# The last third of both down projections in seven products of halves, half of its weight sums on GpSimd

## The chip, the cores and the metric

One core of a Trainium2 chip. The metric is the device time of one execution in microseconds (us); the kernel before takes 1169.24 us, the median of three runs (1168.03 to 1169.33).

## The reference

A hybrid decoder block on 528 tokens (16 learned meta tokens and 512 of input), 1024 channels, float32:

```python
h = h + 0.5 * swiglu(rmsnorm(h, ffn1_norm), w_gate1, w_up1, w_down1)
u = rmsnorm(h, mix_norm)
...
h = h + merged @ w_out
h = h + 0.5 * swiglu(rmsnorm(h, ffn2_norm), w_gate2, w_up2, w_down2)
return rmsnorm(h, final_norm)[:, 16:]

def swiglu(x, w_gate, w_up, w_down):
    return (silu(x @ w_gate) * (x @ w_up)) @ w_down
```

Between the two feed-forwards stands a token mixer (latent attention beside a gated DeltaNet), which the change leaves alone. The hidden width of a feed-forward is 2816.

## The kernel before

Activations lie transposed: channels on the 128 partitions, tokens along the free dimension (528 in the first feed-forward, 512 in the second). 1024 channels are eight such tiles, the hidden width is 22 (`FT`), numbered by `ft`. Every matrix is multiplied at higher accuracy than one pass gives: an operand x is split into hi (a cast to the matmul's format, on ScalarE) and lo = x - hi (on VectorE; `split`, L290 to L292, and L176/L177 for plain weights), and a product is three matmuls, hi hi, hi lo and lo hi (`mm3`, L204).

The function `ffn` (L303) is used for both feed-forwards. Its parts, in the order of the program:

- Plain tiles: the first `2 * nc_` hidden tiles (`NC1 = 3` pairs in the first feed-forward, `NC2 = 2` in the second) have gate and up each computed by `mm3` over eight k-tiles, 48 matmuls of 264 columns (24 of 512 in the second feed-forward). VectorE evicts them times the norm factor r (L386, L390) and multiplies gate by up (L400).
- The forms: all other gate and up tiles are made in pairs of output tiles by Strassen's scheme in Winograd's variant, a 2x2 block product in seven products instead of eight. Blocks are halves: halves of the input channels (four k-tiles each), of the tokens, and the two output tiles. For it the eight input tiles are scaled in place (L407), and for each of four pairs `k`, `k + 4` seven left-hand combinations are formed (L410 to L420): four splits and four subtractions (L413). They stay in SBUF; `xf[p][k]` is the operand of product p.
- A quad (`quad`, L442) is one pair of output tiles of gate (j = 0) or up (j = 1): it loads two raw weight tiles, forms four weight sums s1 to s4 (`side`, L427 to L429, 128x512 on VectorE), splits the seven weight operands (`form`, cast on ScalarE at L291 and difference on VectorE at L292, 128x512 each), and runs seven products of 12 matmuls (`product`, L440). Seven adds on VectorE (L433) combine them from PSUM; one product is first copied by ScalarE (L456).
- Chunks: hidden tiles are finished in three chunks, `CHUNKS1 = ((0, 8), (8, 16), (16, 22))` and `CHUNKS2 = ((0, 6), (6, 14), (14, 22))`. When a chunk is done, its activations are split (`halve`), and its share of the down projection is given out as eight down tiles (`down`, one per output tile m) between the quads of the next chunk, one after each quad; the last chunk's eight run at the end. A down tile is a plain `mm3` over the chunk's k-tiles, accumulated into the residual tile (L345).
- `finish` hands a finished output tile on: in the first feed-forward it stores it, prepares the mixer's operands and adds its square to the next norm; in the second it does the final norm. The norms' squares are added on GpSimd (L251). The last two down tiles of the second feed-forward run in token halves, so that the final norm of the first half starts early.

The program is written with the Tile framework: it allots the buffers of a tag in turn, sets the semaphores, and orders each engine's instructions by a priority that follows the order of the code. Tags that matter here: raw weights four buffers (`wraw`, `wrx`), forms eight (`whi`, `wlo`, `wex`), weight sums three (`sf`).

```python
def side(x, y, op=ALU.subtract):
    t = hid.tile([P, 4, P], F32, tag="sf", name="sf", bufs=NSF)
    nc.vector.tensor_tensor(out=t, in0=x, in1=y, op=op)
    return t
```

Of the kernel before, what the change touches and what calls it, by code (L numbers as in the profile page):

```python
# [17 lines left out]
P = 128  # L18
D = 1024
NT = 528  # L20
# [33 lines left out]
LAG = 3  # L54
NC1 = 3
NC2 = 2
CHUNKS1 = ((0, 8), (8, 16), (16, 22))
CHUNKS2 = ((0, 6), (6, 14), (14, 22))
# [3 lines left out]
NRAW = 4  # L62
NSF = 3
ORD = (2, 0, 3, 1, 4, 5, 6, 7)
ONP = (2, 3)
# [30 lines left out]
def build(tc, a, out, tap=None):  # L96
# [3 lines left out]
    with ctx:  # L100
# [24 lines left out]
        def col(name, i=0):  # L125
            return cols[:, COLS[name] + i:COLS[name] + i + 1]
# [176 lines left out]
        def ffn(wg, wd, xs, hks, wname, r, n, hid, tmp, ra, rb, hk_tile, nc_, load, finish, pre=()):  # L303
# [27 lines left out]

            two = []

            def down(c, m):
                k0, k1 = CHUNKS[c]
                k, last = k1 - k0, c == len(CHUNKS) - 1
                w, x = weights(wd[m, :, k0:k1], k), [hs[ft] for ft in range(k0, k1)]
                if c == 0:
                    hkm[m] = hk_tile(m)[:, 0:n]
                    load(m, hkm[m])  # L340
                ps = mm_tile("dn")
                hk = hkm[m]

                def acc(o, p):
                    nc.vector.scalar_tensor_tensor(out=o, in0=p, scalar=0.5, in1=o, op0=ALU.mult, op1=ALU.add)  # L345

                if last and n == SEQ and m >= KT - 2:
                    two.append((m, ps, w, hk))
                    for y in range(2 if m == KT - 1 else 0):
                        t = slice(y * h, y * h + h)  # L350
                        for m_, p_, w_, hk_ in two:
                            mm3([(p_[:, y, 0:h], y * h, y * h + h)], w_, x, True, True)
                            acc(hk_[:, t], p_[:, y, 0:h])
                            finish(m_, hk_, y)
                    return
                if n == NT:
                    mm3(outs528(ps), w, x, True, True)
                    acc(v2(hk), halves(ps))
                else:
                    mm3([(ps[:, 0, :], 0, n)], w, x, True, True)  # L360
                    acc(hk, ps[:, 0, :])
                if last:
                    finish(m, hk)
# [38 lines left out]
            lhs, rhs = slice(0, h), slice(h, n)  # L402
            xf = {p: [] for p in range(1, 8)}
            for k in range(4):
                x, y = hks[k][:, 0:n], hks[k + 4][:, 0:n]
                for t, kt in ((x, k), (y, k + 4)):
                    nc.vector.scalar_tensor_tensor(out=t, in0=t, scalar=col(wname, kt), in1=r[:, 0:n], op0=ALU.mult, op1=ALU.mult)  # L407
                b, yh, yl = (own(f"b{3 * k + i}", F32R) for i in range(3))
# [8 lines left out]
                for p, hi, lo in ((1, b[:, lhs], b[:, rhs]), (2, yh[:, lhs], yl[:, lhs]), (3, yh[:, rhs], yl[:, rhs]),  # L417
                                  (4, th[:, lhs], tl[:, lhs]), (5, sh[:, lhs], sl[:, lhs]), (6, th[:, rhs], tl[:, rhs]),
                                  (7, sh[:, rhs], sl[:, rhs])):
                    xf[p].append((hi, lo))  # L420

            def m0_tile(name):
                return mm_tile(name)[:, 0, :]

            PT = [{"m": m0_tile, "s": sm_tile, "t": tk_tile, "a": ax_tile}[c] for c in BANKS]

            def side(x, y, op=ALU.subtract):  # L427
                t = hid.tile([P, 4, P], F32, tag="sf", name="sf", bufs=NSF)
                nc.vector.tensor_tensor(out=t, in0=x, in1=y, op=op)  # L429
                return t  # L430
# [10 lines left out]

            def quad(ft, j, o0, o1):  # L442
                raw = []
# [4 lines left out]
                for i in range(2):  # L448
                    nc.sync.dma_start(raw[i], wg[ft + i, j])
                a11, a12, a21, a22 = raw[0][:, 0:4], raw[0][:, 4:8], raw[1][:, 0:4], raw[1][:, 4:8]  # L450
                c1 = tmp.tile([P, NT], F32, tag="cp", name="cp", bufs=NCP)[:, 0:n]
                u2, u3 = c1[:, lhs], c1[:, rhs]
# [3 lines left out]
                nc.scalar.copy(p1, ps)  # L456
                s1 = side(a21, a22, ALU.add)
                s2 = side(s1, a11)
                ps = PT[1]("gu")[:, 0:h]
# [4 lines left out]
                add(o0[:, lhs], ps, p1)  # L464
                s3 = side(a11, a21)
                ps = PT[3]("gu")[:, 0:h]
# [5 lines left out]
                add(u2, ps, u2)  # L472
                s4 = side(a12, s2)
                ps = PT[5]("gu")[:, 0:h]
# [7 lines left out]
            for c, (k0, k1) in enumerate(CHUNKS):  # L482
                nq = max(k1 - max(k0, 2 * nc_), 0)
                given, q = 0, 0
                for ft in range(max(k0, 2 * nc_), k1, 2):
                    gs = [tmp.tile([P, NT], F32, tag="g", name="g", bufs=NG)[:, 0:n] for _ in range(2)]
                    raws.extend(raw_tile(ft + i)[:, 0:n] for i in range(2))
                    for j in range(2):
                        os = (gs, raws[-2:])[j]
                        quad(ft, j, *os)  # L490
                        for i, o in enumerate(os):
                            if j == 0:
                                table(o, o, AF.Silu)
                            else:
                                nc.vector.tensor_tensor(out=o, in0=o, in1=gs[i], op=ALU.mult)
                        q += 1
                        if c:
                            while given < KT * q // nq:
                                down(c - 1, given)
                                given += 1  # L500
                if c == len(CHUNKS) - 1:
                    table_set(LNEXP)
                for ft in range(k0, k1):
                    halve(ft)
            for m in range(KT):
                down(len(CHUNKS) - 1, m)

# [1051 lines left out]
```

## Time and profile before

| | |
|---|---|
| median of three runs | 1169.24 us |
| the profiled execution | 1168.86 us, span 1167.1 us |
| TensorE (PE) busy | 1152.7 us, 99% of the span, 8132 matmuls |
| VectorE (DVE) busy | 859.5 us, 74% |
| ScalarE (ACT) busy | 560.3 us, 48% |
| GpSimd (POOL) busy | 83.0 us, 7% |
| granted TensorE clock | 0.998 of full speed |
| first feed-forward | about 2 to 371 us |
| mixer and its projections | 371 to 806 us |
| second feed-forward and final norm | 806 to 1167 us |

The profile is of one execution. Engines stand there as PE, PEld (weight loads, which overlap PE), DVE, ACT, POOL and SP (the queue that issues most transfers). L440 is line 440 of the kernel; helpers such as `mm3` and `split` put all their operations on one line, so tiles tell more: `gu` is gate or up, `dn` down, `sf` a weight sum, `form` a split weight operand, `hd`, `ut`, `rb` and `ra` are forms of activations. A matmul's recorded length includes its pipeline, so consecutive ones overlap; what a group costs is read from starts.

### The profile page before, as it was taken

How to read it: one execution, taken by the hardware profiler on the slowest of the kernel's cores; microseconds unless marked ns; L12 is line 12 of the kernel's file. 1: busy time of each engine (PE TensorE's matmuls, PEld its weight loads, DVE VectorE, ACT ScalarE, POOL GpSimd, SP SyncE). 2: the span in 40 equal slices, each digit the busy share in tenths (PEclk: the TensorE clock that was granted, in tenths of full speed). 3: DMA queues.
4: the chain of work that ended last, by engine and by line, in shares of the span. 5: the costliest groups of instructions: out<-in, count | busy, mean ns of one | idle time of the engine just before them, and what ended most of it. 6: DMA issues, size and time to landing. Idle time of an engine off the chain costs nothing.

```text
span 1167.1 us, 20801 instructions
## 1 busy us (share of the span) xinstructions
PE 1152.7 (99%) x8132; PEld 1053.9 (90%) x8132; DVE 859.5 (74%) x1588; ACT 560.3 (48%) x989; POOL 83.0 (7%) x108
## 2 busy tenths in 40 slices
PE   9999999999999999999999999999999999999997
PEld 9999999999999989888877888878899999999986
DVE  6998787776665879963786666645999878877744
ACT  7554343533445584365466554434454445433443
POOL 0000000000003221001100000221000000000011
PEclk9999999999999999999999999999999999999999
DMA  6432332333235433445656445555433333323322
GB/s 243 129 124 96 109 104 97 95 94 103 82 101 174 153 89 122 138 148 154 186 157 180 136 131 167 184 178 174 155 105 132 111 93 105 101 100 107 93 71 73
DMA packets 74114, 148.51 MB, mean 127 GB/s; under 512 B 20288, under 2 KB 30864, under 8 KB 74016
## 3 DMA queue, kind: packets, MB, share of 16 engines
q1 hardware_dynamic: 73472, 146.66, 39.9%
q8 instruction: 64, 1.05, 0.4%
q10 hardware_dynamic: 544, 0.52, 0.1%
q14 instruction: 34, 0.28, 0.1%
HBM read 128.56 MB, written 18.60 MB: 126 GB/s over the span
## 4 chain that ended last, share of the span: by engine, by line
PE 94%; DVE 2%; ACT 2%; DMA 1%; issue 1%; SPq 0%; DVEq 0%; ACTq 0%
PE gu L440 30%; PE dn L204 21%; PE gu L204 10%; PE gate L204 8%; PE wo L204 4%; PE mo L204 4%; PE qkv L204 3%; PE z L204 2%; PE s L1169 2%; PE cq L204 1%; ACT dec L150 1%; PE pt L1202 1%; PE o L1231 1%; PE qk L1025 1%; PE vn L996 1%; PE qn L204 1%
## 5 line engine op out<-in xcount | busy, mean ns | idle before, releaser
L176 ACT CAST whi<-wraw 128x1024 fp32r<-128x1024 f32 (+2 forms) x121 | 122.9, 1016 | 174.1 <-issue 66.4
L177 DVE TENSOR_TENSOR wlo<-wraw,whi 128x1024 fp32r<-128x1024 f32 (+2 forms) x121 | 146.5, 1211 | 24.6 <-ACT whi L176 24.4
L440 PE MATMUL gu<-hd,form 128*128 128x256 f32 (+1 forms) x1224 | 164.7, 283 | 0.0
L440 PEld LDWEIGHTS gu<-hd,form 128*128 128x128 f32 x1224 | 155.9, 190 | 1.6
L291 ACT CAST form<-sf 128x512 fp32r<-128x512 f32 x136 | 83.0, 620 | 113.9 <-DVE sf L429 65.7
L440 PE MATMUL gu<-rb,form 128*128 128x256 f32 x864 | 112.6, 283 | 0.0
L345 DVE SCALAR_TENSOR_TENSOR hk<-dn,hk 128x528 f32<-128x528 f32 (+2 forms) x50 | 33.9, 678 | 100.7 <-PE dn L204 100.7
L440 PEld LDWEIGHTS gu<-rb,form 128*128 128x128 f32 x864 | 107.7, 192 | 0.0
L291 ACT CAST form<-wraw 128x512 fp32r<-128x512 f32 x102 | 63.1, 620 | 85.9 <-PE gu L440 56.4
L292 DVE TENSOR_TENSOR form<-sf,form 128x512 fp32r<-128x512 f32 x136 | 92.8, 688 | 12.3 <-ACT form L291 12.1
L440 PE MATMUL gu<-ut,form 128*128 128x264 f32 x768 | 101.1, 284 | 0.0
L204 PE MATMUL dn<-hd,whi 128*128 128x264 f32 (+2 forms) x376 | 99.0, 315 | 0.0
L440 PEld LDWEIGHTS gu<-ut,form 128*128 128x128 f32 x768 | 96.5, 188 | 0.0
L204 PE MATMUL gate<-ut,whi 128*128 128x512 f32 x256 | 86.5, 412 | 1.3 <-DVE gt L1259 1.3
L204 PE MATMUL dn<-ut,whi 128*128 128x512 f32 (+1 forms) x248 | 85.4, 381 | 0.0
L204 PE MATMUL dn<-ra,whi 128*128 128x264 f32 x464 | 85.3, 285 | 0.0
L292 DVE TENSOR_TENSOR form<-wraw,form 128x512 fp32r<-128x512 f32 x102 | 69.8, 687 | 6.4 <-ACT form L291 6.0
L204 PE MATMUL dn<-ut,wlo 128*128 128x512 f32 (+1 forms) x192 | 72.1, 375 | 0.0
L204 PE MATMUL dn<-ra,wlo 128*128 128x264 f32 x352 | 71.6, 285 | 0.0
L204 PEld LDWEIGHTS dn<-ra,whi 128*128 128x128 f32 x464 | 68.5, 189 | 0.0
L204 PEld LDWEIGHTS dn<-hd,whi 128*128 128x128 f32 x376 | 62.9, 189 | 3.9
L204 PE MATMUL qkv<-ut,whi 128*128 128x264 f32 x384 | 65.2, 288 | 0.0
(434 smaller groups left out, 2311.5 us busy)
## 6 DMA issues: line engine op xcount, KB each, us to landing
wraw<-w SPq DMA_DIRECT2D x86, 512.0 KB, 3.3
wraw<-win SPq DMA_DIRECT2D x36, 512.0 KB, 3.5
wraw<-d SPq DMA_DIRECT2D x32, 512.0 KB, 3.7
wraw<-d SPq DMA_DIRECT2D x16, 384.0 KB, 3.2
hk<-xT SPq DMA_DIRECT2D x16, 264.0 KB, 4.4
dec<-growd SPq DMA_DIRECT2D x8, 512.0 KB, 6.2
gated<-gt SPq DMA_DIRECT2D x16, 256.0 KB, 2.0
sg<-gated SPq DMA_DIRECT2D x16, 256.0 KB, 2.9
```

The costliest lines, as they stand in the source:

```text
L150: ins = nc.scalar.activation(*args, **kw).ins
L176: ih = nc.scalar.copy(hi[:, 0:n], raw[:, 0:n])
L177: il = (nc.gpsimd if pool_lo else nc.vector).tensor_tensor(out=lo[:, 0:n], in0=raw[:, 0:n], in1=hi[:, 0:n].bitcast(F32), op=ALU.subtract)
L204: trail.append(nc.tensor.matmul(o, lhsT=w, rhs=x[:, lo_:hi_], start=start and k == 0 and pi == 0, stop=stop and k == n - 1 and pi == 2).ins)
L291: nc.scalar.copy(hi, x)
L292: (eng or nc.vector).tensor_tensor(out=lo, in0=x, in1=hi.bitcast(F32), op=ALU.subtract)
L345: nc.vector.scalar_tensor_tensor(out=o, in0=p, scalar=0.5, in1=o, op0=ALU.mult, op1=ALU.add)
L440: nc.tensor.matmul(ps, lhsT=wt, rhs=xt, start=k == 0 and i == 0, stop=k == 3 and i == 2)
L996: nc.tensor.matmul(psv[:, h], lhsT=X[c][:, h], rhs=rr[:, h], start=True, stop=True)
L1025: nc.tensor.matmul(ps[:, h4], lhsT=hs(kT, h, o, o + n), rhs=hs(qT, h, o, o + n), start=True, stop=True)
L1169: nc.tensor.matmul(ps[:, 0:w], lhsT=Q[h][:, b * P:(b + 1) * P], rhs=K[h][:, k0:k1], start=True, stop=True)
L1202: nc.tensor.transpose(out=ps[:, b * P:(b + 1) * P], in_=Pr[h // 2, b][:, h % 2, NM + c * P:NM + (c + 1) * P], identity=ident)
```

## The change

It sets `NC1` to 2 and the chunks of both feed-forwards to 6, 8, 8 tiles: the first feed-forward has four plain hidden tiles (eight gate and up tiles) instead of six, and nine pairs of quads instead of eight. During the quads of the last chunk only two down tiles (`EARLY`) of the chunk before are given out; four more follow, with the forms of the last chunk's eight activations made between them (`forms`, now a function). Then the last chunk's down projection runs as four quads (`down_quad`), each for two output tiles, with seven products of halves, and the two remaining down tiles of the chunk before come last. The weight sums of the last chunk's gate and up quads go by `QENG`: s1, s2 on VectorE and s3, s4 on GpSimd; those of the down quads by `DENG`: s1 on VectorE, the other three on GpSimd. Each line number of the new code is three to some forty higher than before.

```diff
-NC1 = 3
+NC1 = 2
-CHUNKS1 = ((0, 8), (8, 16), (16, 22))
+CHUNKS1 = ((0, 6), (6, 14), (14, 22))
+EARLY = 2
+QENG = "vvpp"
+DENG = "vppp"
...
+            def down_quad(m):
+                k0, k1 = CHUNKS[-1]
+                os = own("r0", F32)[:, 0:n], ra(7, F32)[:, 0:n]
+                quad([wd[m + i, :, k0:k1] for i in range(2)], *os, own("cd", F32) if n == SEQ else c1_tile(), DENG)
+                for i, o in enumerate(os):
+                    hk = hkm[m + i]
+                    nc.vector.scalar_tensor_tensor(out=hk, in0=o, scalar=0.5, in1=hk, op0=ALU.mult, op1=ALU.add)
...
-            def side(x, y, op=ALU.subtract):
+            def side(x, y, e, op=ALU.subtract):
                 t = hid.tile([P, 4, P], F32, tag="sf", name="sf", bufs=NSF)
-                nc.vector.tensor_tensor(out=t, in0=x, in1=y, op=op)
+                (nc.gpsimd if e == "p" else nc.vector).tensor_tensor(out=t, in0=x, in1=y, op=op)
...
-                s3 = side(a11, a21)
+                s3 = side(a11, a21, eng[2])
...
-                            while given < KT * q // nq:
+                            while given < (EARLY if sevens and c == len(CHUNKS) - 1 else KT) * q // nq:
                                 down(c - 1, given)
                                 given += 1
...
-            for m in range(KT):
-                down(len(CHUNKS) - 1, m)
+            for k in range(4):
+                down(ending, EARLY + k)
+                forms(k, raws[CHUNKS[-1][0] + k], raws[CHUNKS[-1][0] + 4 + k])
+            for m in range(EARLY + 4, KT - 2):
+                down(ending, m)
+            for m in range(0, KT, 2):
+                down_quad(m)
+                if n == SEQ and m < KT - 2:
+                    for i in range(2):
+                        finish(m + i, hkm[m + i])
+            if n == NT:
+                for m in range(KT - 2):
+                    finish(m, hkm[m])
+            for m in range(KT - 2, KT):
+                down(ending, m)
```

`sevens` is always true, and `ending` is the last chunk but one. What moves on the engines, at three places:

VectorE before, at the end of the forms for the first feed-forward's first quad. `gu_745` and `gu_804` are plain tiles (two more plain tiles follow `gu_745` on TensorE), `ut_997` is the last form of the activations, `form_1013` and `form_1034` belong to the first quad's products 1 and 6:

```order
L429 TENSOR_TENSOR sf_1031<-sf_1029,wraw_1006 128x512
L429 TENSOR_TENSOR sf_1067<-wraw_1006,wraw_1007 128x512
L292 TENSOR_TENSOR ut_997<-hk_116,ut_996 128x528
L390 TENSOR_TENSOR hd_687<-gu_745,r_213 128x528
L292 TENSOR_TENSOR form_1013<-wraw_1006,form_1013 128x512
L400 TENSOR_TENSOR hd_687<-g_686,hd_687 128x528
L292 TENSOR_TENSOR form_1034<-sf_1031,form_1034 128x512
L390 TENSOR_TENSOR g_802<-gu_804,r_213 128x528
```

VectorE after, at the same place. `gu_629` is the last plain tile; `form_781` and `form_819` belong to products 1 and 2 of the first quad, and product 6's split stands two rows behind the piece:

```order
L406 TENSOR_TENSOR hd_571<-gu_629,r_213 128x528
L295 TENSOR_TENSOR ut_744<-hk_115,ut_743 128x528
L416 TENSOR_TENSOR hd_571<-g_570,hd_571 128x528
L429 TENSOR_TENSOR hk_112<-hk_112 128x264
L295 TENSOR_TENSOR form_781<-wraw_775,form_781 128x512
L429 TENSOR_TENSOR hk_112<-hk_116,hk_112 128x264
L451 TENSOR_TENSOR sf_797<-wraw_776 128x512
L429 TENSOR_TENSOR hk_116<-hk_116,hk_112 128x264
L295 TENSOR_TENSOR ut_763<-hk_112,ut_762 128x528
L429 TENSOR_TENSOR hk_116<-hk_116 128x264
L451 TENSOR_TENSOR sf_799<-sf_797,wraw_775 128x512
L295 TENSOR_TENSOR form_819<-wraw_775,form_819 128x512
```

Before, the last form stood ahead of two evictions of plain tiles; now eleven operations and more stand behind the last plain tile's eviction before the first quad's second product has its operand.

TensorE after, at the first quad of the first feed-forward (products 1, 2 and 6 write `gu_780`, `gu_818` and `gu_801`):

```order
L207 MATMUL gu_629<-ra_171,wlo_632 128x264 x2
L462 MATMUL gu_780<-hd_688,form_781 128x264 x2
L462 MATMUL gu_818<-hd_689,form_819 128x264
L462 MATMUL gu_818<-hd_690,form_819 128x264
L462 MATMUL gu_780<-hd_688,form_781 128x264
L462 MATMUL gu_780<-hd_709,form_781 128x264 x3
L462 MATMUL gu_780<-hd_730,form_781 128x264 x3
L462 MATMUL gu_780<-hd_751,form_781 128x264 x3
L462 MATMUL gu_818<-hd_689,form_819 128x264
L462 MATMUL gu_801<-ut_701,form_802 128x264
L462 MATMUL gu_801<-ut_702,form_802 128x264
```

Before, each of a quad's products stood as twelve matmuls in a row from the first quad on; now products are taken in pieces of one to eleven in the first three quads, and whole after that.

GpSimd before, at the end of the second feed-forward, where it has the norm's adds alone:

```order
L251 TENSOR_TENSOR sqa_12789<-sq_12717,sq_12752 128x512
L251 TENSOR_TENSOR sqa_12826<-sqa_12789,sq_12787 128x512
L251 TENSOR_TENSOR sqa_12863<-sqa_12826,sq_12824 128x512
L251 TENSOR_TENSOR sqa_12900<-sqa_12863,sq_12861 128x512
L1456 TENSOR_TENSOR sq5_12942<-sqa_12900,sq_12898 128x512
```

GpSimd after, in the second feed-forward's last two down quads (each has three sums):

```order
L451 TENSOR_TENSOR sf_13176<-sf_13174,wraw_13152 128x512
L451 TENSOR_TENSOR sf_13212<-wraw_13152,wraw_13153 128x512
L254 TENSOR_TENSOR sqa_13141<-sq_12995,sq_12998 128x512
L451 TENSOR_TENSOR sf_13249<-wraw_13152,sf_13176 128x512
L451 TENSOR_TENSOR sf_13324<-sf_13322,wraw_13300 128x512
L254 TENSOR_TENSOR sqa_13146<-sqa_13141,sq_13139 128x512
L451 TENSOR_TENSOR sf_13360<-wraw_13300,wraw_13301 128x512
L254 TENSOR_TENSOR sqa_13289<-sqa_13146,sq_13144 128x512
L451 TENSOR_TENSOR sf_13397<-wraw_13300,sf_13324 128x512
L254 TENSOR_TENSOR sqa_13294<-sqa_13289,sq_13287 128x512
```

The norm's adds now stand between the weight sums in one queue; in the first feed-forward all norm adds come behind the last sum.

## Rows read from the trace of the kernel before

**Rows 1.** The page: busy time by engine, and the chain that ended last.
```profile
PE 1152.7 (99%) x8132; PEld 1053.9 (90%) x8132; DVE 859.5 (74%) x1588; ACT 560.3 (48%) x989; POOL 83.0 (7%) x108
...
PE 94%; DVE 2%; ACT 2%; DMA 1%; issue 1%; SPq 0%; DVEq 0%; ACTq 0%
```

**Rows 2.** The chain in order of time, first feed-forward: start us, length us, what.
```profile
25.73 52.57 PE gu L204 x436
78.29 30.60 PE gu L440 x252
108.89 5.85 PE dn L204 x48
114.74 10.22 PE gu L440 x84
...
237.48 5.88 PE dn L204 x48
...
370.66 4.01 PE misc L204 x33
```

**Rows 3.** The same chain, second feed-forward.
```profile
1001.07 10.06 PE gu L440 x84
1011.13 5.58 PE dn L204 x24
```

**Rows 4.** Busy time by stretch, first feed-forward; PE, PEld, DVE, ACT, POOL, clock, DMA.
```profile
30.00:54.90 24.90, 24.90 (x209) 24.90 (x208) 24.90 (x41) 12.09 (x19) 0.00 (x0) 1.00 0.44 136
...
78.30:108.90 30.60, 30.60 (x254) 30.60 (x254) 30.38 (x58) 16.01 (x29) 0.00 (x0) 1.00 0.33 104
109.00:237.00 128.00, 128.00 (x1054) 128.00 (x1053) 98.37 (x176) 53.59 (x88) 0.00 (x0) 1.00 0.31 100
```

**Rows 5.** VectorE in time from 29 us: start, length, operation, [idle before, releaser].
```profile
29.89 0.71 DVE L376 TENSOR_TENSOR g<-g,r 128x528 f32<-128x528 f32 x1
30.51 0.70 DVE L376 TENSOR_TENSOR hd<-hd,r 128x528 f32<-128x528 f32 x1
...
32.37 1.22 DVE L177 TENSOR_TENSOR wlo<-wraw,whi 128x1024 fp32r<-128x1024 f32 x1
33.50 0.70 DVE L390 TENSOR_TENSOR hd<-gu,r 128x528 f32<-128x528 f32 x1
...
35.87 1.45 DVE L407 SCALAR_TENSOR_TENSOR hk<-hk,cols,r 128x528 f32<-128x528 f32 x2
37.23 0.43 DVE L292 TENSOR_TENSOR hd<-hk,hd 128x264 fp32r<-128x264 f32 x1
...
72.55 0.71 DVE L390 TENSOR_TENSOR g<-gu,r 128x528 f32<-128x528 f32 x1 [2.01 <-PE gu L204]
```

**Rows 6.** VectorE in time, one quad among the later ones.
```profile
134.00 0.43 DVE L433 TENSOR_TENSOR cp<-gu,p 128x264 f32<-128x264 f32 x1
134.34 0.68 DVE L429 TENSOR_TENSOR sf<-sf,wraw 128x512 f32<-128x512 f32 x1
134.94 0.69 DVE L292 TENSOR_TENSOR form<-wraw,form 128x512 fp32r<-128x512 f32 x1
...
146.93 0.71 DVE L345 SCALAR_TENSOR_TENSOR hk<-dn,hk 128x528 f32<-128x528 f32 x1 [4.46 <-PE dn L204]
```

**Rows 7.** GpSimd in time, merging of the branches and the end.
```profile
739.94 1.29 POOL L1411 TENSOR_TENSOR sg<-sg,sg 128x512 f32<-128x512 f32 x1 [4.27 <-DVE sg L1410]
...
752.14 2.15 POOL L1411 TENSOR_TENSOR sg<-sg,sg 128x512 f32<-128x512 f32 x1 [5.36 <-DVE sg L1410]
...
1145.94 1.31 POOL L1456 TENSOR_TENSOR sq<-sqa,sq 128x512 f32<-128x512 f32 x1 [4.20 <-ACT sq L238]
```

**Rows 8.** VectorE in time beside the first two of these.
```profile
740.11 2.21 DVE L177 TENSOR_TENSOR wlo<-wraw,whi 128x1024 fp32r<-128x1024 f32 x1 [0.31 <-ACT whi L176]
...
751.92 1.21 DVE L177 TENSOR_TENSOR wlo<-wraw,whi 128x1024 fp32r<-128x1024 f32 x1
```

**Rows 9.** VectorE in time beside the third.
```profile
1146.92 0.42 DVE L345 SCALAR_TENSOR_TENSOR hk<-dn,hk 128x256 f32<-128x256 f32 x1 [2.13 <-PE dn L204]
```

More of the change, by code (lines that the diff above doesn't have):

```diff
@@ L332, in ffn, with c1_tile @@
             two = []
+            sevens = True
+            ending = len(CHUNKS) - 1 - sevens
+            def c1_tile():
+                return tmp.tile([P, NT], F32, tag="cp", name="cp", bufs=NCP)[:, 0:n]
+            def down_quad(m):
[5 more added lines that the diff above has]
+                    nc.vector.scalar_tensor_tensor(out=hk, in0=o, scalar=0.5, in1=hk, op0=ALU.mult, op1=ALU.add)
             def down(c, m):
                 k0, k1 = CHUNKS[c]
-                k, last = k1 - k0, c == len(CHUNKS) - 1
+                k = k1 - k0
                 w, x = weights(wd[m, :, k0:k1], k), [hs[ft] for ft in range(k0, k1)]
@@ L345, in acc @@
                     nc.vector.scalar_tensor_tensor(out=o, in0=p, scalar=0.5, in1=o, op0=ALU.mult, op1=ALU.add)
-                if last and n == SEQ and m >= KT - 2:
+                if c == ending and n == SEQ and m >= KT - 2:
                     two.append((m, ps, w, hk))
@@ L361, in down @@
                     acc(hk, ps[:, 0, :])
-                if last:
+                if c == ending and (not sevens or m >= KT - 2):
                     finish(m, hk)
@@ L402, in ffn, with forms @@
             lhs, rhs = slice(0, h), slice(h, n)
[L403 to L407, printed above, removed]
+            xf = {}
+            def forms(k, x, y):
+                if k == 0:
+                    xf.update((p, []) for p in range(1, 8))
                 b, yh, yl = (own(f"b{3 * k + i}", F32R) for i in range(3))
@@ L420, in ffn @@
                     xf[p].append((hi, lo))
+            for k in range(4):
+                x, y = hks[k][:, 0:n], hks[k + 4][:, 0:n]
+                for t, kt in ((x, k), (y, k + 4)):
+                    nc.vector.scalar_tensor_tensor(out=t, in0=t, scalar=col(wname, kt), in1=r[:, 0:n], op0=ALU.mult, op1=ALU.mult)
+                forms(k, x, y)
             def m0_tile(name):
@@ L440, in product, with quad @@
                         nc.tensor.matmul(ps, lhsT=wt, rhs=xt, start=k == 0 and i == 0, stop=k == 3 and i == 2)
-            def quad(ft, j, o0, o1):
+            def quad(srcs, o0, o1, c1, eng):
                 raw = []
@@ L448, in quad @@
                 for i in range(2):
[L449 removed]
+                    nc.sync.dma_start(raw[i], srcs[i])
                 a11, a12, a21, a22 = raw[0][:, 0:4], raw[0][:, 4:8], raw[1][:, 0:4], raw[1][:, 4:8]
[L451 removed]
                 u2, u3 = c1[:, lhs], c1[:, rhs]
@@ L456, in quad @@
                 nc.scalar.copy(p1, ps)
-                s1 = side(a21, a22, ALU.add)
-                s2 = side(s1, a11)
+                s1 = side(a21, a22, eng[0], ALU.add)
+                s2 = side(s1, a11, eng[1])
                 ps = PT[1]("gu")[:, 0:h]
@@ L472, in quad @@
                 add(u2, ps, u2)
-                s4 = side(a12, s2)
+                s4 = side(a12, s2, eng[3])
                 ps = PT[5]("gu")[:, 0:h]
@@ L489, in ffn @@
                         os = (gs, raws[-2:])[j]
-                        quad(ft, j, *os)
+                        quad([wg[ft + i, j] for i in range(2)], *os, c1_tile(), QENG if sevens and c == len(CHUNKS) - 1 else "vvvv")
                         for i, o in enumerate(os):
@@ L502, in ffn @@
                     table_set(LNEXP)
+                    if sevens:
+                        break
                 for ft in range(k0, k1):
                     halve(ft)
-            for m in range(KT):
-                down(len(CHUNKS) - 1, m)
+            if not sevens:
+                for m in range(KT):
+                    down(len(CHUNKS) - 1, m)
+                return
+            for k in range(4):
+                down(ending, EARLY + k)
[12 more added lines that the diff above has]
+                down(ending, m)
         xs = []
```

## The prediction, made before the change was run

> **What bounds the kernel now.** The page comes first: TensorE is busy for 99% of the span and holds 94% of the chain that ended last [rows 1]. VectorE's 74% is an average over stages, so I read it by stage. The chain in order of time [rows 2, 3] shows both feed-forwards as unbroken TensorE work. A quad (84 matmuls, four weight tiles' worth of output in seven products) takes 10.22 us in the first feed-forward and 10.06 in the second; a down tile of eight k-tiles takes 5.85 to 5.88 and 5.58; the plain gate and up tiles run 436 matmuls in 52.57 us, 0.1206 us each. The granted clock is 1.00 throughout [rows 4], so no term below is a clock term. The same windows show where VectorE is no cover: from 30 to 54.9 us it is busy for all of 24.90 us, against 98.4 of 128 us among the later quads. Its own timeline [rows 5] shows why: it scales the eight input tiles, builds their seven forms and evicts plain tiles in one uninterrupted row from 29.89 us, and first waits for TensorE at 70.5 us (the row at 72.55, idle 2.01 us before it). TensorE reaches its first quad only at 78.29.
>
> From [rows 5, 6] come VectorE's steps, start to start, which is what a full queue costs: a 128x528 operation 0.62 us (29.89 to 30.51), a scaling 0.68 (two in 35.87 to 37.23), a 128x1024 weight split 1.13 (32.37 to 33.50), a 128x264 operation 0.34 (134.00 to 134.34), a 128x512 split or sum 0.60 (134.34 to 134.94).
>
> **What TensorE saves.** The first feed-forward drops four plain tiles, 4 x 48 x 0.1206 = 23.15 us, and gains two quads, 20.44: 2.7 us less. In both, eight down tiles of the last chunk become four quads: 8 x 5.86 - 4 x 10.22 = 6.0 us less in the first, 8 x 5.58 - 4 x 10.06 = 4.4 less in the second. There the gain is smaller since one 512-wide matmul (5.58 / 24 = 0.2325) costs less than two of 256 (10.06 / 84 = 0.1198 each). The second feed-forward has its four plain tiles and its chunks already, so that half of the change does nothing there. Sum: 13.1 us less TensorE work.
>
> **What the earlier start of the quads costs.** With four tiles fewer, TensorE is ready for the first quad at 78.29 - 23.15 = 55.1 us, and would finish the third at 108.89 - 23.15 = 85.7. In the changed order VectorE still has, from the row at 29.89 to the split that product 7 of the third quad waits for, 108 operations: 3 weight splits x 1.13 + 8 scalings x 0.68 + 32 x 0.62 + 34 x 0.345 + 31 x 0.60 = 59.0 us, so that split ends at 88.9. After it TensorE has 44 matmuls of the quad left, 5.4 us: 94.4 with the hand-over. Loss: 94.4 - 85.7 = 8.7 us. The removed plain tiles took with them only four weight splits, four evictions and two products of VectorE's. Bounds: 5.7 if only the first quad is late (by the same count its product 2 waits for a split at 62.3, its product 3 for one at 69.3, and it would end at 70.9 instead of 65.3) and the lead is regained after; 10 if ScalarE's casts fall behind too, about a microsecond in all. I take 8.7, since VectorE's row in [rows 5] has no gap in which to regain anything. Afterwards a quad plus a six-deep down tile (10.22 + 4.39) leaves VectorE idle, as it is now: 4.46 us before the row at 146.93 [rows 6].
>
> **The second set of forms.** The last chunk's eight activations become left operands of seven products: four splits and four subtractions for each of four pairs, in place of eight splits. From the end of the last gate/up quad to product 6 of the first down quad VectorE has 14 x 0.62 + 13 x 0.345 + 3 x 1.13 + 4 x 0.60 = 19.0 us in the first feed-forward. It lies under five down tiles in a row, 29.3 us: nothing. In the second it is 23.6 us and three GpSimd sums under 27.9: nothing, with little to spare. Without that cover it would be lost whole.
>
> **The sums on GpSimd.** None of these exists before, so I use the nearest rows. A 128x512 GpSimd add takes 1.29 us (start 739.94) [rows 7], and a VectorE weight split beside it takes 2.21 instead of 1.21 [rows 8]: it began 0.17 us after the add and ended 1.09 us after it. The other way round (start 752.14) the GpSimd add takes 2.15. They take turns, for whole instructions. A VectorE operation that reads PSUM passes: 0.42 us at 1146.92 [rows 9] inside a GpSimd add that runs from 1145.94 to 1147.25. So a sum that leaves VectorE (0.60) can hold it for 1.29.
>
> The Trainium skill (SBUF — State Buffer, section "Who interferes with whom") says the same: a VectorE instruction with two SBUF inputs and a GpSimd instruction that reads SBUF lock each other out for the whole instruction, and one with a single SBUF input is not touched. By it the move is worth less than nothing where VectorE is full; without it each moved sum would simply free 0.60 us. The trace agrees, by the 2.21 us above.
>
> Gate/up quads of the last chunk, first feed-forward: VectorE has 7 splits + 2 sums at 0.60, 7 adds at 0.345 and a product at 0.62: 8.4 us, plus two holds, 2.6: 11.0 against TensorE's 10.22. Eight of them with the two down tiles (3.5) and eight splits of the chunk before (5.0) are 96.8 us against 87.6. That is 9.2 late at worst, less the one quad (8.4) that VectorE is ahead: 0.8. At best the adds lie beside the holds: 8.6 per quad, nothing. I take nothing. Down quads: splits for three quads (the first one's are made before) and adds and accumulations for four are 3 x 4.8 + 4 x 3.7 = 29.2 us. In the second feed-forward GpSimd also has the norm's adds: 13 holds x 1.29 = 16.8. Together 46.0 against 40.2: 5.8 at worst, nothing if the 28 adds (9.7 us) all lie beside holds. I take a quarter, 1.4 us; in the first feed-forward, without norm adds, nothing.
>
> **What costs nothing.** Loads: as many and as large as before (44 gate/up and 24 down tiles each), in a queue that is a third busy [rows 4]. The four buffers give a quad's loads a whole quad to land. In the first feed-forward the norms of six outputs move behind the last quad, under two down tiles (11.7 us) against six casts and six squares on ScalarE and five GpSimd adds of at most 2.15 us [rows 7]. The end of the kernel keeps its two halved down tiles.
>
> **Sum.** The profiled execution takes 1168.86 us (span 1167.1), 0.4 under the median 1169.24. 1168.86 - 13.1 + 8.7 + 1.4 = 1165.9, against the median **1166.2 us**. A measurement of this kernel tells 0.2% (2.3 us) from no change: faster is below 1166.9, slower above 1171.6. The forecast's own range, with the bounds above, is 1162 to 1174.
>
> **Rivals.**
> *The late start doesn't reach TensorE* (0.10). The products of two quads can be interleaved, as the changed order does. For it: VectorE waits 2 us for TensorE before 72.55. Against: every interleaved product still ends on a late split. Time: 1169.2 - 13.1 + 1.4 = 1157.5.
> *The lock drains the lead* (0.10): the other side. GpSimd wins every turn and no add lies beside a hold. Worst-case debts against TensorE: gate/up quads 9.2 and about 10, down quads 4 x (12.4 - 10.22) = 8.9 and 4 x (14 - 10.06) = 16: 44 us in four stages, against leads of one quad each, 4 x 8.4 = 34. It decides as soon as the leads are less than the debts. With half the leads 27 us are lost, of which the spare cover of the first transition (29.3 - 19.0) takes back 10: 1169.2 - 13.1 + 8.7 + 17 = 1181.8. For it: every pair of such rows takes turns. Against: VectorE idles each time it waits for a product's end, and holds cost nothing there.
> This last one is what the skill's SBUF rule would make of the kernel if nothing were ahead.
>
> **Chances.** Forecast 0.80 (of it 0.40 faster, 0.32 same, 0.08 slower: the sum lies just over the border). With the rivals: faster 0.50, same 0.32, slower 0.18. Range 1159 to 1174: the forecast's own range and, below it, the part of the first rival in which the first quad is still somewhat late; the rest of that rival and all of the second, under 2 in 10, are left out.
>
> **What would show it.** TensorE's first quad should start near 55 us, and the third end near 94 with gaps ended by VectorE's splits. The first feed-forward should end where it did (370.5 against 370.66), the whole gain lying in the second. The last quads should run at 10.2 and 10.1 us. I am wrong if the third quad ends by 88 (first rival), or if quads with GpSimd sums take over 10.6 us (second).

## The result, and the profile after

The changed kernel takes **1182.22 us** (median of four runs, 1181.12 to 1183.13) beside 1169.28 us for the kernel before on the same chip: a ratio of 1.0114, with a 95% interval of 1.01 to 1.0128. The forecast was 1166.2, with a range of 1159 to 1174: the kernel became slower and not faster, and the result lies outside the range. The profiled execution has a span of 1179.0 us against 1167.1, so 11.9 us are to be explained, plus the 13.1 us that TensorE was to save.

The page of the changed kernel, busy time by engine and the chain's shares, to set beside [rows 1]:

```profile
PE 1149.9 (98%) x8204; PEld 1054.7 (89%) x8204; DVE 950.4 (81%) x1736; ACT 585.2 (50%) x1065; POOL 163.4 (14%) x164
...
DVE 3%; PE 1%; issue 1%; ACT 1%; POOL 0%; DVEq 0%; POOLq 0%
```

VectorE rose by 91 us, GpSimd by 80. The chain is no longer an unbroken row of TensorE work: followed back from the end it breaks off after 6% of the span, near 1109 us, and in that piece VectorE has the largest share.

**The start.** TensorE in time, first feed-forward of the changed kernel (start, length, operation, [idle before, releaser]); the rows with an idle time of over 0.5 us, the first of the quads and the first behind the third quad:

```profile
54.21 0.65 PE L462 MATMUL gu<-hd,form 128*128 128x264 f32 x4
58.13 2.57 PE L462 MATMUL gu<-hd,form 128*128 128x264 f32 x10 [3.27 <-DVE form L295]
61.60 0.59 PE L462 MATMUL gu<-hd,form 128*128 128x264 f32 x1 [0.90 <-DVE form L295]
84.11 2.08 PE L462 MATMUL gu<-hd,form 128*128 128x264 f32 x12 [0.57 <-DVE hd L455]
88.37 0.39 PE L462 MATMUL gu<-hd,form 128*128 128x264 f32 x1 [2.19 <-DVE form L295]
97.01 0.41 PE L207 MATMUL dn<-ra,whi 128*128 128x264 f32 x2
```

Its stretches, in the columns of [rows 4]:

```profile
54.20:58.10 3.90, 0.66 (x6) 0.45 (x4) 3.90 (x9) 1.26 (x2) 0.00 (x0) 0.84 0.36 84
58.10:62.00 3.90, 2.97 (x11) 2.54 (x11) 3.76 (x8) 1.90 (x4) 0.00 (x0) 0.50 0.37 108
62.00:66.60 4.60, 4.56 (x21) 4.38 (x21) 2.79 (x5) 2.86 (x6) 0.00 (x0) 0.50 0.26 73
66.60:84.00 17.40, 16.94 (x137) 16.72 (x136) 16.75 (x34) 6.22 (x12) 0.00 (x0) 0.99 0.36 114
84.00:97.00 13.00, 10.62 (x82) 10.20 (x83) 12.96 (x25) 6.72 (x12) 0.00 (x0) 1.00 0.31 88
```

Three quads run from 54.21 to 97.01, 42.8 us in place of 30.6 [rows 2]. The long waits end on splits of VectorE, as forecast. What was not forecast stands in the clock column: after the wait of 3.27 us the granted clock is 0.50, the lower of its two levels (1.2 GHz), from 58 to 66.6 us, and ten matmuls take 2.57 us. The slow TensorE in its turn holds up VectorE, which waits 2.02 us for a product and makes the later splits later:

```profile
66.81 0.43 DVE L455 TENSOR_TENSOR cp<-gu,p 128x264 f32<-128x264 f32 x1 [2.02 <-PE gu L462]
```

Not every long wait is followed by a fall: from 84 to 97 us, with a wait of 2.19 us inside, the granted clock is 1.00.

**The last chunks.** Six stretches of four quads each (gate and up quads, the same, down quads; first feed-forward, then second), from the first matmul of the first quad to the first matmul behind the last. Above the changed kernel, below the first experiment, which has all weight sums on VectorE:

```profile
203.80:247.80 44.00, 41.85 (x339) 41.23 (x338) 42.67 (x70) 22.32 (x41) 11.49 (x7) 1.00 0.31 97
253.70:294.60 40.90, 40.90 (x338) 40.90 (x337) 37.27 (x67) 23.77 (x41) 6.97 (x6) 1.00 0.37 109
323.80:366.00 42.20, 41.26 (x338) 41.05 (x337) 37.38 (x61) 21.17 (x37) 14.81 (x13) 1.00 0.41 130
993.20:1036.50 43.30, 41.35 (x338) 40.53 (x337) 41.52 (x68) 21.46 (x41) 10.58 (x7) 1.00 0.32 105
1042.00:1083.70 41.70, 40.87 (x338) 40.42 (x338) 37.24 (x66) 21.67 (x39) 8.16 (x6) 1.00 0.34 108
1111.60:1156.20 44.60, 41.55 (x338) 40.56 (x337) 40.89 (x61) 22.98 (x40) 19.10 (x14) 1.00 0.22 67
```

```profile
203.30:244.25 40.95, 40.95 (x338) 40.95 (x337) 40.37 (x78) 20.57 (x38) 0.00 (x0) 1.00 0.35 117
250.10:291.10 41.00, 41.00 (x339) 41.00 (x338) 38.22 (x75) 24.27 (x41) 0.00 (x0) 1.00 0.41 124
320.30:361.30 41.00, 41.00 (x339) 41.00 (x338) 36.81 (x68) 21.37 (x37) 4.55 (x4) 1.00 0.40 130
988.50:1028.80 40.30, 40.30 (x337) 40.30 (x336) 39.14 (x76) 18.84 (x36) 0.00 (x0) 1.00 0.36 117
1034.40:1074.70 40.30, 40.30 (x338) 40.30 (x336) 37.29 (x74) 22.39 (x40) 0.00 (x0) 1.00 0.39 120
1102.60:1142.90 40.30, 40.30 (x338) 40.30 (x336) 37.73 (x67) 22.83 (x40) 8.59 (x5) 1.00 0.23 70
```

The widths add up to 256.7 us above and 243.85 below: the changed kernel loses 12.9 us there, at a clock of 1.00. Without GpSimd's sums TensorE has no gap at all. By the records VectorE has 45 operations fewer in the stretches above (393 against 438) and is yet busy 7.4 us longer (236.97 against 229.56). At 0.60 us for a sum [rows 6] the operations that stayed took 7.4 + 45 x 0.60 = 34.4 us longer (an estimate from these rows).

What happens is seen at single rows. GpSimd in time, two of its sums:

```profile
194.11 1.29 POOL L451 TENSOR_TENSOR sf<-wraw 128x512 f32<-128x512 f32 x1 [192.79 <-DMA wraw<-w]
...
1122.56 1.29 POOL L451 TENSOR_TENSOR sf<-wraw 128x512 f32<-128x512 f32 x1 [0.63 <-DVE form L295]
```

VectorE in time, the operations beside them, and one that waits for GpSimd:

```profile
194.16 1.79 DVE L451 TENSOR_TENSOR sf<-wraw 128x512 f32<-128x512 f32 x1
...
1119.20 0.69 DVE L451 TENSOR_TENSOR sf<-wraw 128x512 f32<-128x512 f32 x1 [1.14 <-POOL sf L451]
...
1122.74 1.66 DVE L295 TENSOR_TENSOR form<-wraw,form 128x512 fp32r<-128x512 f32 x1
```

A sum that takes 0.68 alone takes 1.79, and ends 0.55 us after GpSimd's; a split that takes 0.69 alone takes 1.66 and also ends 0.55 us after. In the first case the two sums started 0.05 us apart. In the six stretches 37 of GpSimd's 44 weight sums have a VectorE operation of over 1 us beside them that takes about 0.7 alone. VectorE's adds that read PSUM are not touched: their largest group takes 421 ns each in the changed kernel and 422 with all sums on VectorE.

The rest of the account, from starts of TensorE's rows: the first feed-forward's last two down tiles take 12.8 us (366.03 to 378.84) in place of 11.7, with one wait of 0.79 us for a weight split. Together: -13.1 saved, +11.3 at the start (the third quad ends at 97.0 instead of 85.7: 12.2 us more for three quads, of which TensorE was ready 0.9 us earlier than reckoned), +12.9 in the last chunks, +1.1 for these two tiles, -0.3 in the mixer: 11.9 us, as measured. The first feed-forward ends at 378.84 us; 370.5 was forecast.

### The profile page after: what moved, and what is told of

It is laid out like the page before. It is cut to its first block, busy times and chain, and to the rows that moved or that the text cites. A ratio compares the mean times of both kernels' runs of the same rounds, so it can differ in the third digit from the quotient of the medians.

```text
span 1179.0 us, 21285 instructions
## 1 busy us (share of the span) xinstructions
PE 1149.9 (98%) x8204; PEld 1054.7 (89%) x8204; DVE 950.4 (81%) x1736; ACT 585.2 (50%) x1065; POOL 163.4 (14%) x164
## 5 line engine op out<-in xcount | busy, mean ns | idle before, releaser
L462 PE MATMUL gu<-hd,form 128*128 128x264 f32 (+1 forms) x1584 | 218.5, 286 | 15.7 <-DVE form L295 6.4
L462 PEld LDWEIGHTS gu<-hd,form 128*128 128x128 f32 x1584 | 203.6, 192 | 20.6 <-DVE form L295 7.4
L295 DVE TENSOR_TENSOR form<-sf,form 128x512 fp32r<-128x512 f32 x176 | 139.4, 797 | 11.9 <-ACT form L294 11.1
L462 PE MATMUL gu<-ut,form 128*128 128x264 f32 x1056 | 141.7, 286 | 0.0
L462 PEld LDWEIGHTS gu<-ut,form 128*128 128x128 f32 x1056 | 134.8, 190 | 0.3 <-ACT form L294 0.3
L451 POOL TENSOR_TENSOR sf<-wraw 128x512 f32<-128x512 f32 x24 | 37.1, 1547 | 423.5 <-DMA wraw<-w 378.2
L451 DVE TENSOR_TENSOR sf<-wraw 128x512 f32<-128x512 f32 x64 | 49.2, 769 | 11.9 <-DMA wraw<-w 7.0
L207 PEld LDWEIGHTS gate<-ut,whi 128*128 128x128 f32 x256 | 45.9, 189 | 11.7 <-DVE gt L1299 3.0
L207 PEld LDWEIGHTS qkv<-ut,whi 128*128 128x128 f32 x384 | 53.8, 188 | 0.7
L207 PE MATMUL gate<-ut,wlo 128*128 128x512 f32 x128 | 53.1, 415 | 0.0
```

Source lines behind the costliest of these rows:

```text
L207: trail.append(nc.tensor.matmul(o, lhsT=w, rhs=x[:, lo_:hi_], start=start and k == 0 and pi == 0, stop=stop and k == n - 1 and pi == 2).ins)
L295: (eng or nc.vector).tensor_tensor(out=lo, in0=x, in1=hi.bitcast(F32), op=ALU.subtract)
L451: (nc.gpsimd if e == "p" else nc.vector).tensor_tensor(out=t, in0=x, in1=y, op=op)
L462: nc.tensor.matmul(ps, lhsT=wt, rhs=xt, start=k == 0 and i == 0, stop=k == 3 and i == 2)
```

## The experiments

**Theory L**: a weight sum on GpSimd keeps VectorE's operations with two SBUF inputs waiting for its whole length, so in the last chunks VectorE gets less time from the move, not more. **Theory S**: with four plain tiles VectorE has the forms ready too late for the first quads. **Theory C**: the start also pays for a fallen clock. Rivals: **F**, VectorE is too full there whoever makes the sums; **B** and **Q**, the sums come late from GpSimd (too few buffers, or a queue and a handshake).

### All sums back on VectorE, and each half of it

```diff
-QENG = "vvpp"
-DENG = "vppp"
+QENG = "vvvv"
+DENG = "vvvv"
```

> All sums of weights back on VectorE; chunks, plain tiles and the down products in halves stay. Theory L (a sum on GpSimd keeps VectorE's two-input operations out for its 1.29 us, where VectorE's own sum takes some 0.69): VectorE gets 2 x 0.6 us per gate or up quad and 3 x 0.6 us per down quad back, the quads of both last chunks come to 10.2 and 10.1 us, TensorE's 14.3 us of loss there go: 1168 us, and the mean of the splits falls from 0.80 back to 0.69. Rival F (VectorE has too much to do there whoever makes the sums, and GpSimd takes 2 to 3 sums off it): each quad 1.4 to 2.1 us longer, over 1200 us.

Measured: 1168.29 us (ten runs; 0.9997 of before, 0.9988 to 1.0006). F is out. The six stretches are those shown above.

With the first line alone (gate and up):

> Only the gate and up quads' sums back on VectorE, the down quads keep three on GpSimd. Theory L: the 3.2 us (first feed-forward) and 4.4 us (second) that the sixteen gate and up quads lost go: 1174.6 us. Rival F: 16 x 1.4 us more, 1204. Rival B (not the lock, but GpSimd's sums come late because only three buffers stand for them): about 1174.6 too.

Measured: 1173.82 us (1.0046, 1.0029 to 1.0063). With the second line alone (down):

> Only the down quads' sums back on VectorE, the gate and up quads keep two on GpSimd. Theory L: the 1.3 + 1.1 us of the first feed-forward and 4.3 us of the second go: 1175.5 us. Rival F: 8 x 2.1 us more, 1199.

Measured: 1175.11 us (1.0057, 1.0042 to 1.0072). Set against the changed kernel's 1182.22, taking the sums off GpSimd wins 8.4 us in the gate and up quads and 7.1 in the down quads; both together win 13.9, so they nearly add.

### More buffers for the sums

```diff
-NSF = 3
+NSF = 5
```

> Five buffers for the sums in place of three, all else as changed. Theory L: the holds stay, 1182 us within 1.5. Rival B (GpSimd's sums wait for a free buffer behind the matmuls that read the old ones, and come late): the losses of the last chunks go, 1168 us.

Measured: 1190.54 us (1.0186, 1.0171 to 1.0201), which neither theory had. The groups of VectorE's weight sums say which wait went; first the changed kernel, then this one (count, busy, mean ns, idle before and its releasers):

```profile
L451 DVE TENSOR_TENSOR sf<-wraw 128x512 f32<-128x512 f32 x64 | 49.2, 769 | 11.9 <-DMA wraw<-w 7.0 <-POOL sf L451 4.6
```

```profile
L451 DVE TENSOR_TENSOR sf<-wraw 128x512 f32<-128x512 f32 x64 | 45.8, 715 | 9.7 <-DMA wraw<-w 7.1 <-DMA wraw<-d 2.0
```

B saw something real: VectorE's waits for GpSimd's sums, 4.6 us, are gone with five buffers, and ScalarE's, 54.7 us in all in the changed kernel, are down to 5.9. But the time did not come back, so these waits were not what TensorE lost by. The 8.3 us more are in part clock: the three quads at the start, where no sum is on GpSimd, take 46.1 us, with a granted clock of 0.80 from 84 us on. The six stretches of the last chunks take 262.1 us in place of 256.6, two of them at a clock of 0.96. What else made the rest, the order of sums and splits on VectorE for one, was not tried.

### GpSimd's work without its use

All sums on VectorE, and the 56 sums that GpSimd had made once more on GpSimd, into a tile that nobody reads:

```diff
-                (nc.gpsimd if e == "p" else nc.vector).tensor_tensor(out=t, in0=x, in1=y, op=op)
+                nc.vector.tensor_tensor(out=t, in0=x, in1=y, op=op)
+                if e == "p":
+                    s = hid.tile([P, 4, P], F32, tag="scr", name="scr")
+                    nc.gpsimd.tensor_tensor(out=s, in0=x, in1=y, op=op)
```

> All sums on VectorE as in the run that had every sum back there (1168.3 us), and beside each of the 56 that the change gave to GpSimd the same sum once more on GpSimd, into a tile that nobody reads: the work of GpSimd without any use of its results. Theory L (a GpSimd sum holds VectorE's two-input operations, whoever needs the sum): VectorE has all its own sums and the holds on top, each quad of the last chunks loses 0.7 to 1.9 us (gate, up) or 1 to 2.5 (down): 1187 to 1215 us, and the splits' mean rises from 0.69 to 0.8 or more. Rival Q (the changed kernel loses because sums come late from GpSimd, 1.3 us behind a queue, and the splits behind them): nobody waits for these, so 1168.3 within 1.5.

Measured: 1201.64 us (1.028, 1.0267 to 1.0293). This is the run that decides: no engine uses those sums, and they cost 33.3 us against the same kernel without them, 0.6 us each. Nobody waits for these sums, so lateness (Q) cannot be what they cost. They do keep the raw weights in use for longer, but the group of VectorE's sums that reads raw weights waits 6.4 us for loads here instead of 4.2. With the run of five buffers, Q is out as the main cause in the changed kernel too. The largest group of VectorE's splits, in the run with all sums on VectorE and here:

```profile
L295 DVE TENSOR_TENSOR form<-sf,form 128x512 fp32r<-128x512 f32 x176 | 120.0, 689 | 9.2 <-ACT form L294 8.4
```

```profile
L295 DVE TENSOR_TENSOR form<-sf,form 128x512 fp32r<-128x512 f32 x176 | 137.6, 789 | 8.5 <-ACT form L294 7.6
```

That is 100 ns more on each of 176 splits, 17.6 us, in this group alone; in the changed kernel the mean is 797 ns. Some of the 33.3 us is again clock: in two of this run's six stretches it is 0.96 and 0.93.

### The start alone

The kernel before, with:

```diff
-NC1 = 3
+NC1 = 2
-CHUNKS1 = ((0, 8), (8, 16), (16, 22))
+CHUNKS1 = ((0, 6), (6, 14), (14, 22))
```

> The kernel before with only the first feed-forward's start changed: four plain tiles, chunks of 6, 8, 8; no halves in the down tiles, nothing on GpSimd. Theory S (VectorE cannot have the forms ready when TensorE is through with four plain tiles): TensorE saves 2.7 us of plain tiles and loses 11 to 12 us in the first three quads, and also pays about as much for its down products as before: 1168.7 + 8.6 = 1177.3 us. Rival (the early quads only lose there because the rest of the change disturbs them, or the loss is made good later): 1166 to 1169 us.

Measured: 1179.11 us (1.0081, 1.0067 to 1.0096), 1.8 us more than expected. The three quads take 44.7 us here, with a clock of 0.50 from 58 to 66.6 us and 0.89 from 84 on: two waits were followed by a fall, not one. The second wait is 2.17 us long, as long as the one in the changed kernel that no fall followed; why they differ is open. S holds, and nothing is made good later: the quads behind run at 10.24 us each.

### Matmuls nobody reads, in the first gap

All sums on VectorE, and in the first product of the first quad:

```diff
+                        if p == 1 and n == NT and not kept and (k, i) == (1, 0):
+                            kept.append(mm_tile("dn")[:, 0, 0:h])
+                            for _ in range(KEEP):
+                                nc.tensor.matmul(kept[0], lhsT=f[:, 0], rhs=xf[1][0][0], start=True, stop=True)
```

> Four plain tiles, all sums on VectorE (as in the run that had every sum back on VectorE), and 26 matmuls of 128x264 more, whose result nobody reads, in the gap of 3.3 us that TensorE has after the first matmuls of the first quad. Theory C (beside VectorE's lateness the start pays for the granted clock, which falls to 0.5 after that gap and stays there to 66 us): the clock stays at 1.0, VectorE no longer waits for TensorE near 65 us, the third quad ends some 2 us earlier, 1166 us. Rival (VectorE alone sets the third quad's end): 1168.3, or some tenths more if the extra matmuls run past the gap.

Measured: 1167.09 us (0.9983, 0.9974 to 0.9991). The stretches that answer to those of the start above:

```profile
54.20:58.10 3.90, 3.36 (x28) 3.15 (x26) 3.90 (x9) 1.27 (x2) 0.00 (x0) 1.00 0.37 90
58.10:62.00 3.90, 2.35 (x17) 2.13 (x18) 3.90 (x9) 2.61 (x5) 0.00 (x0) 1.00 0.34 99
62.00:66.60 4.60, 4.60 (x40) 4.60 (x39) 4.60 (x10) 2.41 (x6) 0.00 (x0) 1.00 0.28 79
66.60:84.00 17.40, 16.31 (x130) 15.66 (x128) 17.12 (x34) 7.52 (x14) 0.00 (x0) 1.00 0.32 114
```

The clock stays at 1.00. TensorE gets 40 matmuls done between 62 and 66.6 us, where it got 23 at a clock of 0.58 in the run with all sums on VectorE (21 in the changed kernel). VectorE's wait for a product near 66 us, 1.53 us in that run, is gone, and the third quad ends at 94.38 instead of 96.48. C holds for the profiled execution, by the 2.1 us expected. The medians differ by 1.2; the profiled execution is the shortest of the eleven (1165.23), and the others were not looked into.

### Six plain tiles again

```diff
-NC1 = 2
+NC1 = 3
```

> The changed kernel with six plain tiles again, so the first chunk has no quads; down halves and GpSimd sums stay. Theory S: the 11.3 us of the start go and the two plain tiles give back 2.7: 1182.2 - 8.6 = 1173.6 us. Rival: within 2 us of 1182.

Measured: 1177.71 us (1.0073, 1.006 to 1.0086): faster than the change, as S has it, but 4 us above the number. The start is as good as expected: the first quads come at 77.97 us and take 10.22 each. The profiled execution, the longest of the four (1179.82), shows two things that the number left out. The six stretches of the last chunks add up to 261.4 us from starts instead of 256.6, so what the holds cost depends on where they fall; why they fall worse here is open. And the mixer takes 438.8 us instead of 434.6, with a granted clock of 0.69 and 0.63 from 570 to 580 us behind a wait of only 0.48 us; the last experiment comes back to this place.

With all sums on VectorE as well:

> Both losses taken out: six plain tiles, all sums of weights on VectorE, chunks of 6, 8, 8 and the down tiles of the last chunk in halves. If the two losses are separate they add: 1168.3 - 8.6 = 1159.7 us, 0.992 of the kernel before. If the one hides the other: above 1165.

Measured: **1159.74 us** (seven runs, 1158.72 to 1166.34; 0.994, 0.9919 to 0.9961), as expected; that the median meets the number so closely is partly luck in a spread as wide as this. It beats both kernels: it keeps the part of the change that saves (the down tiles in halves) without the two that cost.

### The same sums, where VectorE has time

The last version with `QENG` at "vvpp" again, and:

```diff
-QENG if sevens and c == len(CHUNKS) - 1 else "vvvv"
+QENG if c == 1 else "vvvv"
```

> The fastest version so far (six plain tiles, all sums on VectorE in the last chunks, 1159.7 us) with two sums of each quad of the middle chunk, not of the last one, on GpSimd. Between those quads stands a plain down tile each, 14.6 us of TensorE per quad and tile (14.3 in the second feed-forward), where VectorE has 11.9 us of work by its share of 81 per cent. Theory L (a hold costs time only where VectorE has none to spare): two holds add 1.2 us, VectorE stays under 14.6, 1159.7 within 1. Rival Q (sums from GpSimd come late wherever they are): some 0.4 us per quad as in the last chunks, 16 quads, 1166.

Measured: 1162.55 us (four runs, 1159.47 to 1164.51; 0.9949, 0.9935 to 0.9964): 2 us above the bound that was set, 3.5 below Q. The spread of such runs, below, bears on this median. Its profiled execution, the shortest of the four with a span of 1157.7, shows the quads of both middle chunks (in the second feed-forward with the two quads before them), and the splits:

```profile
77.50:194.50 117.00, 117.00 (x962) 117.00 (x961) 98.43 (x158) 50.33 (x85) 20.82 (x14) 1.00 0.30 98
844.40:979.90 135.50, 134.89 (x986) 127.91 (x985) 119.75 (x200) 61.54 (x108) 24.31 (x16) 1.00 0.33 103
```

```profile
L295 DVE TENSOR_TENSOR form<-sf,form 128x512 fp32r<-128x512 f32 x168 | 127.3, 764 | 2.8 <-ACT form L294 2.4
```

The holds are there (764 ns, against 684 in the version without). The first stretch takes as long as in that version, the second 1.1 us longer (135.5 against 134.4). In the last chunks the same move of two sums per quad costs 7.3 us by the profile, from starts: 3.0 and nothing in the two halves of the first feed-forward, 2.9 and 1.3 in the second. So L holds in kind, if not to the microsecond: most of what a hold takes is lost only where VectorE has none to spare (it is busy for 84 and 88% of the two stretches here).

### The norms' sums too

The version with six plain tiles and all weight sums on VectorE, and:

```diff
-            norm2 = Norm(fp, NT, "nm")
-            norm3 = Norm(fp, SEQ, "nf")
+            norm2 = Norm(fp, NT, "nm", None, nc.vector)
+            norm3 = Norm(fp, SEQ, "nf", None, nc.vector)
```

> The fastest version so far (1159.7 us), with the sums of squares that the last down tiles of both feed-forwards give to GpSimd on VectorE too. In the down quads of the second feed-forward TensorE still waited 0.5 us there, behind VectorE operations of 3.2 and 1.8 us beside such sums. Theory L: these waits go, at most 0.5 us, 1159.2 to 1159.7 us. Rival (seven to fourteen more VectorE operations of 0.7 us in the same quads are too many): 1161 us or more.

Measured: 1159.67 us (six runs; 0.9929, 0.9912 to 0.9947). The wait of 0.51 us in the last down quads is gone (40.53 us for four instead of 41.06); the medians do not tell the two versions apart. The same kernel was run once more, for the spread of its runs:

> The version with all sums, those of squares too, on VectorE, once more as it is. Its six runs fell into two groups: four of 1158.4 to 1159.8 us at a mean granted clock of 0.997 to 0.999, two of 1164.6 at 0.993. Theory D (in some executions TensorE has one longer wait, after which the granted clock stands at its lower level for a stretch, as at the start of the changed kernel): if the profiled run is of the second group, its rows show one such stretch, some 5 to 6 us longer than in the first. Rival (the whole execution is a little slower): no stretch differs by more than 1 us. If the profiled run is of the first group, this stays open.

Measured: 1158.80 us (four runs, 1158.71 to 1164.02; 0.9914, 0.9896 to 0.9932). The profiled execution was the one of 1164.02, span 1162.2 against 1157.7. All feed-forward stretches agree within 0.2 us; the mixer takes 440.3 us instead of 435.4. Its place, TensorE's row and the stretches around it:

```profile
563.12 0.51 PE L207 MATMUL qn<-cqh,whi 128*128 128x512 f32 x1 [1.59 <-ACT qn L1174]
```

```profile
560.00:565.00 5.00, 3.41 (x29) 2.67 (x25) 3.19 (x8) 3.52 (x10) 0.12 (x1) 1.00 0.81 230
565.00:570.00 5.00, 5.00 (x24) 4.66 (x24) 1.64 (x3) 1.22 (x2) 1.27 (x1) 0.50 0.40 122
570.00:575.00 5.00, 5.00 (x38) 4.18 (x38) 3.04 (x11) 0.59 (x1) 0.00 (x0) 0.82 0.01 3
```

In the execution profiled before, this wait is not there and the clock is 1.00 in all three stretches. D holds here: one wait, and the lower level behind it. The length of the wait alone doesn't tell whether the clock falls: in the run with six plain tiles and GpSimd's sums it fell at the same place behind 0.48 us. ScalarE had stood behind an operation of GpSimd that came 1.4 us later than in the other execution; what made that late was not followed further.

## Why the prediction was wrong

**The step that failed** is "The sums on GpSimd": "I take nothing" for the gate and up quads and "a quarter, 1.4 us" for the down quads. By the runs those sums cost 13.9 us (1182.22 - 1168.29): 8.4 and 7.1 taken singly. The mechanism was read rightly from [rows 7, 8]. The debts at worst were large enough (9.2 and about 10 us for the gate and up quads, 5.8 for the second down quads), but what was left of them was not: after a lead of 8.4 us the first feed-forward's gate and up quads were to lose 0.8 us at most, and they lost 3.0; its down quads were to lose nothing, and they lost 1.2. In the second feed-forward the two lost 4.3 each. Two assumptions set these values.

First, that the debt of a chunk is spread over its eight quads and the lead of one quad pays for it. TensorE's waits in the first feed-forward's last chunk stand in its first three quads, here as rows of the changed kernel; the second four lost nothing (253.70 to 294.60, above; in the second feed-forward they lost 1.3 us):

```profile
214.45 1.70 PE L462 MATMUL gu<-hd,form 128*128 128x264 f32 x12 [0.23 <-DVE cp L455]
...
218.50 1.73 PE L462 MATMUL gu<-hd,form 128*128 128x264 f32 x12 [0.88 <-DVE g L455]
...
230.07 1.69 PE L462 MATMUL gu<-hd,form 128*128 128x264 f32 x12 [1.04 <-DVE hd L455]
```

The eight splits of the chunk before (5.0 us) fall into the first quad, on top of its holds: on VectorE they start between 203.53 and 213.27 us. The lead is spent by 214 us, and a loss that has happened is not paid back by the quads that follow.

Second, that adds from PSUM would lie beside the holds and make them free. They pass, but they stand in one queue with the splits, and beside 37 of the 44 sums an operation with two SBUF inputs came up and was held. The 34.4 us that VectorE's remaining operations took longer are 0.8 us for each of the 44 GpSimd sums in the six stretches (53 records less the norms' nine), against the 0.60 us that a moved sum frees. So VectorE had more to do after the move than before it.

Here the rule of the Trainium skill (SBUF — State Buffer, section "Who interferes with whom"), that a VectorE instruction with two SBUF inputs and a GpSimd instruction that reads SBUF contend for an exclusive lock, should have had the weight of the forecast. The traces agree with it at the rows at 194.16 and 1122.74, and the run with the unused sums prices it at 33.3 us. I had it as a rival at 0.10.

**The start**: forecast 8.7 us lost, the third quad's end at 94.4; measured 11.3. It ended at 97.01 in the changed kernel, 96.48 with all sums on VectorE and 94.38 where the clock was kept up. The count of VectorE's 108 operations was right: where the clock was kept up, the last of them ends at 88.8 us (88.9 reckoned), from a start at 29.15 us instead of 29.89. TensorE's last wait, though, ends on an earlier split of the same quad, and the 108th came in time. Wrong was the sentence that with a clock of 1.00 in [rows 4] "no term below is a clock term": the row showed a TensorE without gaps, and the change makes gaps. By these ends that is 2.1 to 2.6 us.

**TensorE's saving**, 13.1 us: right. With all sums on VectorE the last quads run in 10.24 and 10.08 us without a gap, and with the start mended too the time falls by 9.2 (1168.94 to 1159.74), against 10.4 for the down tiles alone.

**The second set of forms**, at nothing: right; down quads start without a wait in that run. **The down tiles behind the last quad**: their 1.1 us (a split 0.79 us late) was not forecast. It is there with all sums on VectorE as well and not with six plain tiles, and its cause is open.

**The rivals.** That the late start would not reach TensorE (1157.5) is out. The second, at 1181.8, comes nearest to what happened, and its mark was met: the down quads of the second feed-forward take 44.6 / 4 = 11.1 us, over the 10.6 that was set. But its premise that no add lies beside a hold is not what the rows show, and its closeness is partly luck: it had 17 us for the lock, where 13.9 were measured, and nothing for the clock and the two down tiles.

## What to carry to other kernels

Moving work from a full VectorE to GpSimd pays only if the moved operation frees more VectorE time than it holds up; price both from rows, and count a debt where it falls in the queue, not over the stage. Where a change makes TensorE wait for the first time, put a fallen clock behind the wait into the bounds of the sum: rows without gaps say nothing of it. When a change has several parts, the one that saves may do better alone: here the down tiles in halves, with six plain tiles and all sums on VectorE, 1159.7 us.

## What the runs showed that I had not expected

- A wait of TensorE of 3.27 us was followed by some 8 us at the lower clock level, and one of 1.59 us in the mixer by a fall to the same level from 565 us to past 570. The second, wait and fall together, made the mixer 4.9 us longer, and so made the difference between the two profiled executions of one and the same kernel, 1159.5 and 1164.0 us. Other waits of 2.2 us were followed by a fall in one run and by none in another.
- 26 matmuls that nobody reads, in a gap of 3.3 us, made the kernel faster (1167.09 against 1168.29 us, medians of eleven and ten runs).
- Five buffers instead of three for the weight sums made the kernel 8.3 us slower, and the start, where GpSimd has no sums, is 3.3 us of it (46.1 against 42.8 us, in the profiled executions).
- The same move of two sums per quad costs 7.3 us in the last chunks and 1.1 us in the middle ones, both by the profiled executions.
